# Score matmuls of a two-branch attention layer: the lower halves of q of both components in one block, on two halves of TensorE's rows

## The chip, the core and the metric

One core of a Trainium2 chip. A core has five engines that run their own instruction streams: TensorE (PE; its weight loads are shown apart as PEld), VectorE (DVE), ScalarE (ACT), GpSimd (POOL) and SyncE (SP, here the issuer of almost all DMAs). TensorE multiplies a stationary block of up to 128 rows x 128 columns with a moving block of up to 512 columns and adds into PSUM, which has eight banks. The metric is the device time of one execution in microseconds; lower is better. All times are of the whole kernel.

## What is computed

One layer of a streaming encoder: 2048 prompt rows (16 tiles of 128) and 128 sample rows (8 sequences of 16, one further tile), width 1024. After adaLN modulation one projection gives q, k, v and gates of two attention branches, A and B; both are merged, projected and normed.

```python
def diff_attention(q, k, v, qpos, kpos, lam):            # A: 4 heads, 2 components of 64
    s = jnp.einsum('bqhcd,bkhcd->bhcqk', q, k) * (HEAD_DIM_A ** -0.5)
    mask = (kpos // CHUNK)[None, :] <= (qpos // CHUNK)[:, None]
    p = jax.nn.softmax(jnp.where(mask, s, -jnp.inf), axis=-1)
    w = p[:, :, 0] - lam * p[:, :, 1]
    return jnp.einsum('bhqk,bkhe->bqhe', w, v)

def stick_breaking_attention(q, k, v, qpos, kpos):        # B: 8 heads of 64
    z = jnp.einsum('bqhd,bkhd->bhqk', q, k) * (HEAD_DIM_B ** -0.5)
    mask = kpos[None, :] < qpos[:, None]
    log_1m = jnp.where(mask, jax.nn.log_sigmoid(-z), 0.0)
    log_a = jax.nn.log_sigmoid(z) + lax.cumsum(log_1m, axis=3, reverse=True) - log_1m
    a = jnp.where(mask, jnp.exp(log_a), 0.0)
    return jnp.einsum('bhqk,bkhd->bqhd', a, v)
```

Inputs and outputs are float32. The kernel gets near that precision from float16 by halves: a value x is scaled and split into an upper half, x rounded to float16, and a lower half, the rounding error, and a product of two values is taken as upper x upper + upper x lower + lower x upper.

## The kernel before, in words

**Units.** The work is cut into eight units u of two *components* of 64 dimensions: even u is a head of A (its two components c = 0, 1), odd u two heads of B (one component each). For every unit the 17 tiles are taken in the order sample tile (t = NT = 16), then t = 0 to 15. A step is one (unit, tile).

**What a step does.** `project` (from L407) multiplies a tile of the modulated input with the unit's weights in 24 matmuls of 512 columns (L428) and, for the gates, 24 more (L504). Its `finish` splits q, k and v into halves on ScalarE (upper) and VectorE (lower): `halves` and `query`, L456 to L463. A's q and k are rotated on POOL before that. `transpose_qk` (L512) turns q and k with TensorE into one bank of PSUM (tag `t`) and copies them out (L531, L532): on ScalarE for A, on VectorE for B. `scores` (L625) goes over chunks of 512 keys, of which a tile t has t // 4 + 1, the last (diagonal) one of 128 to 512 columns with a mask that is added by one more matmul (L643). `evacuate` (L549) takes a chunk's scores out of PSUM: for A on VectorE with a running maximum (L558), for B as two sigmoids on ScalarE (L119), the second in place, which `stick` then reads in a scan on VectorE (L616). After the last chunk come softmax and weights (A: `softmax_pair`) or the products on POOL (B: `stick_weights`, L622), a split, a transpose by DMA (`turn`), and two steps later the multiplication with v (`pv_block`, L696 to L701).

**The score matmul.** `k16` holds for each component c the 128 columns [upper k | lower k], so that its transpose, block c of `kst`, has upper k on rows 0 to 63 and lower k on rows 64 to 127. `qbuf` holds four blocks of 128: for each c the upper q twice, [upper q | upper q], and for each c [lower q | zeros]; the zeros are written once at the start by POOL (L398). One matmul over 128 rows (L639) gives upper q x upper k + upper q x lower k; the second (L640), over 128 rows too, adds lower q x upper k and multiplies the lower k with zeros.

**PSUM.** Eight banks of 512 float32 columns: two of tag `mm` (projection), three of `s` (scores), one of `t` (transposes, gates), two of `o` (PV). A bank is taken in turn when `bank(tag)` is called; the first matmul into it waits until the last reader of its former content is done. In A one chunk of one component takes one `s` bank.

**Order.** `interleave` (L91) merges, for each step, three lists of pieces: projections taken from a line that runs about five steps ahead, the chunks of `scores`, and the PV blocks of the step two before. Each piece has a cost, and a piece is placed by the middle of its cost within its list's total. On top of this the framework's scheduler, which works with a model of times, may move instructions of an engine past one that is not ready in its model; on the chip each engine then runs its list in order.

**Tail.** After the eight units come the branch and output projections (L1315, L1344), and beside them the sample rows (`sample`, L722), whose q, k and v halves were put into DRAM (`s_d`, L491 and L534) during the units and are read back (`fetch`, L734). `queries` (L740) spreads the samples' q over a padded tile `qpad`, so that the scores over the cached keys run as matmuls of 32 columns of TensorE (L772); `scores_all` (L756) does these and the scores over the samples' own keys, both components of which share one `s` bank. `s` banks also serve the transposes of the tail (L1163).

Of the kernel before, what the change touches and what calls it, by code (L numbers as in the profile page):

```python
# [109 lines left out]
def layer_kernel(ctx: ExitStack, tc: tile.TileContext, a: dict):  # L110
# [54 lines left out]
    g_d = [dram.tile([P, 2 * D], F32, name=f"g_d{t}") for t in range(NT + 1)]  # L165
    s_d = [dram.tile([P, 8, P], F16, name=f"s_d{u}") for u in range(8)]
    gate_d = dram.tile([9, D], F32, name="gate_d")
# [227 lines left out]
    qs = c01.enter_context(tc.tile_pool(name="qs", bufs=1))  # L395
    qbuf = [qs.tile([P, 2, 2, 2, 64], F16, name=f"qbuf{i}") for i in range(2)]
    for qb in qbuf:
        G.memset(qb[:, 1, :, 1, :], 0.0)  # L398
    silu_z = {}
# [7 lines left out]
    def project(U, t):  # L407
# [30 lines left out]
        def finish():  # L438
# [17 lines left out]
            def halves(dst, src, scale):  # L456
                src = src.rearrange("p (c d) -> p c d", d=64)
                split(dst[:, :, 0, :], dst[:, :, 1, :], src, scale, S)

            def query(src, scale):  # L460
                src = src.rearrange("p (c d) -> p c d", d=64)
                S.activation(out=qb[:, 0, :, :, :], in_=src.unsqueeze(2).to_broadcast([P, 2, 2, 64]), func=AF.Identity, scale=scale)
                V.scalar_tensor_tensor(out=qb[:, 1, :, 0, :], in0=src, scalar=scale, in1=qb[:, 0, :, 0, :], op0=ALU.mult, op1=ALU.subtract)  # L463
            if kind == 0:
                cosT, sinT = box["r"][:, 0:32], box["r"][:, 32:96]
                x4 = pr[:, 0:256].rearrange("p (c f d) -> p c f d", c=4, f=2)
                rot = stg.tile([P, 256], F32, tag="rot", name="rot")
                r2 = stg.tile([P, 256], F32, tag="r2", name="r2", bufs=1)
                G.tensor_tensor(out=rot.rearrange("p (c f d) -> p c f d", c=4, f=2), in0=x4,
                                in1=cosT.unsqueeze(1).unsqueeze(1).to_broadcast([P, 4, 2, 32]), op=ALU.mult)  # L470
                G.tensor_tensor(out=r2.rearrange("p (c f d) -> p c f d", c=4, f=2), in0=x4[:, :, ::-1, :],
                                in1=sinT.rearrange("p (f d) -> p f d", f=2).unsqueeze(1).to_broadcast([P, 4, 2, 32]),
                                op=ALU.mult)
                G.tensor_tensor(out=rot, in0=rot, in1=r2, op=ALU.add)
                halves(vt, p[:, 256:384], s2)
                query(rot[:, 0:128], s)
                halves(k16, rot[:, 128:256], s)
            else:
                rot = pr
                halves(vt, p[:, 256:384], s2)  # L480
                halves(k16, p[:, 128:256], s2)
                query(p[:, 0:128], s2)
# [7 lines left out]
            if t == NT:  # L490
                load(out=s_d[U["u"]][:, 6:8, :], in_=vt.rearrange("p c f d -> p c (f d)"))  # L491
            U["q16", t], U["k16", t] = qb, k16
# [19 lines left out]
    def transpose_qk(U, t):  # L512
        g, i = t // 4, t % 4
        q16, k16 = U.pop(("q16", t)), U.pop(("k16", t))
        pt = bank("t", F16)
        for c in range(2):
            T.transpose(pt[:, c * P : (c + 1) * P], k16[:, c, :, :].rearrange("p f d -> p (f d)"), id16)
        for f in range(2):
            for c in range(2):
                j = 2 + f * 2 + c  # L520
                T.transpose(pt[:, j * P : (j + 1) * P], q16[:, f, c, :, :].rearrange("p r d -> p (r d)"), id16)
        if t == NT:
            sam = stg.tile([P, 6, P], F16, tag="sam", name="sam", bufs=1)
            qst, kst = sam[:, 0:4, :], sam[:, 4:6, :]
        else:
            if i == 0:
                U["k"][g] = kvp.tile([P, 2, 512], F16, tag="k", name="k", bufs=K_BUFS)
            U["q", t] = qst = stg.tile([P, 4, P], F16, tag="qst", name="qst", bufs=Q_BUFS)
# [3 lines left out]
        copy(out=qst, in_=pt[:, 256:768].rearrange("p (j n) -> p j n", j=4))  # L532
        if t == NT:
            load(out=s_d[U["u"]][:, 0:6, :], in_=sam)  # L534

# [89 lines left out]
    def scores(U, t, jobs):  # L625
# [5 lines left out]

        def chunk(c, ch):
            job = own[c if kind == 1 else 0]
            seg = job["segs"][ch * 4 // SEG]
            n = 512 if ch < t // 4 else (t % 4 + 1) * P
            p = bank("s")
            qst, kk = U["q", t], U["k"][ch]
            diag = ch == t // 4
            T.matmul(p[:, 0:n], qst[:, c, :], kk[:, c, 0:n], start=True, stop=False)  # L639
            T.matmul(p[:, 0:n], qst[:, 2 + c, :], kk[:, c, 0:n], start=False, stop=not diag)  # L640
            if diag:
                m = mask_a if kind == 0 else mask_b
                T.matmul(p[:, n - m.shape[1] : n], idb, m, start=False, stop=True)  # L643
            evacuate(job, seg, c, p, ch * 512 - seg["lo"] * P, n, sc[:, 3:4], sc[:, 4:5], ch)
            if kind == 0:
                if diag and c == 1:
# [20 lines left out]
        return ([(0.1, silu)] if kind == 1 else []) + [(2.0 if ch < t // 4 else (t % 4 + 1) / 2, lambda c=c, ch=ch: chunk(c, ch)) for c, ch in order]  # L667

# [53 lines left out]
    def sample(U, dec, qpad, cs):  # L722
# [16 lines left out]

        def queries():  # L740
            for r in range(2):
                V.tensor_copy(out=qpad.rearrange("p j (i r) n -> p j i r n", r=2)[:, :, :, r, r * NS : (r + 1) * NS],
                              in_=box["s"][:, 0:4, :].rearrange("p j (i r s) -> p j i r s", r=2, s=NS)[:, :, :, r, :])

# [11 lines left out]
        def scores_all():  # L756

            box["jobs"] = [new_job(U, t, c, 5, dec) for c in range(heads)]
            qsam, kn = box["s"][:, 0:4, :], box["s"][:, 4:6, :]
            mask = mask_as if kind == 0 else mask_bs  # L760
            pn = bank("s")
            for c in range(2):
                p = pn[:, c * P : (c + 1) * P]
                T.matmul(p, qsam[:, c, :], kn[:, c, 0:P], start=True, stop=False)
                T.matmul(p, qsam[:, 2 + c, :], kn[:, c, 0:P], start=False, stop=False)
                T.matmul(p, idb, mask, start=False, stop=True)
            for c in range(2):
                pc = bank("s")
                for b in range(2):
                    for f in range(2):  # L770
                        for i in range(4):
                            T.matmul(pc[i * 32 : i * 32 + 32, :], qpad[:, f * 2 + c, 2 * i + b, :], box["k", i][:, b * 4 : b * 4 + 4, c, :],  # L772
                                     start=(b == 0 and f == 0), stop=(b == 1 and f == 1))
                job = box["jobs"][c % heads]
                seg = job["segs"][0]
                evacuate(job, seg, c, pn[:, c * P : (c + 1) * P], 512, P, sc[:, 3:4], sc[:, 4:5], 1)
                evacuate(job, seg, c, pc, 0, 512, box["f"][:, 0:1], box["f"][:, 1:2], 0)
                if kind == 1:
                    stick(seg, None, 512, P, pn[:, c * P : (c + 1) * P])
                    stick(seg, None, 0, 512, pc)  # L780
# [27 lines left out]
        def finish():  # L808
            po = bank("s")
            vn = box["s"][:, 6:8, :].rearrange("p c (f d) -> p c f d", f=2)  # L810
            for job in box["jobs"]:
# [615 lines left out]
```

## Time and profile before

| | |
|---|---|
| median of 3 runs | 2341.11 us (2338.23 to 2343.4) |
| profiled execution: span | 2337.1 us |
| matmuls, and as many weight loads | 15272 |
| mean rate of DMA | 191 GB/s, 445.35 MB |
| score matmuls L639 and L640 | 640 each |
| transposes of k (L517) and q (L521) | 272 and 544 |

The span runs from the first to the last instruction of the profiled execution; the lowest of the runs, which are timed from outside, is 1.1 us above it, the median 4.0 us; the profiled execution has no other time of its own. L12 is line 12 of the kernel before. Busy shares are shares of the span; a matmul's shown duration is longer than its share of TensorE's time, since matmuls follow each other before the one ahead has ended, so the distance between starts is what counts for a row of matmuls.

### The profile page before, as it was taken

The numbers are of one execution on the slowest core, as the hardware profiler recorded it, in microseconds if no ns is written. First come the engines' busy times: TensorE is split into PE (matmuls) and PEld (weight loads), VectorE is DVE, ScalarE is ACT, GpSimd is POOL, SyncE is SP. The second block draws the span as 40 slices with busy tenths as digits, with TensorE's granted clock in tenths as the row PEclk, the third lists the DMA queues.
The fourth block names the chain that finished last, engine by engine and source line by source line (L and its number), as shares of the span: only waits on it lengthen the run. The fifth ranks groups of instructions, "written<-read, shape, count | busy, mean of one in ns | idle before, by whom it ended". The sixth has DMA issues, their size and how long they took to land. (4 is left out here: it accounts for less than half of the span.)

```text
span 2337.1 us, 42708 instructions
## 1 busy us (share of the span) xinstructions
PE 2121.6 (91%) x15272; PEld 1144.0 (49%) x15272; DVE 1707.5 (73%) x3653; ACT 1663.1 (71%) x3292; POOL 661.3 (28%) x578
## 2 busy tenths in 40 slices
PE   5998898998989899899999979999995878989998
PEld 3654454545545445445545545554553444544443
DVE  4658765779875677978667797777788777777663
ACT  4968777787877778778677777866777656756541
POOL 1222022356300334731024474103345111121111
PEclk7999999999999999999999999999997988999999
DMA  9777659897895898867577777756677999999521
GB/s 333 275 214 180 152 118 272 179 193 168 212 210 126 216 204 192 179 178 192 134 191 176 185 168 186 195 146 150 146 171 166 285 254 233 257 245 236 155 98 53
DMA packets 834358, 445.35 MB, mean 191 GB/s; under 512 B 537210, under 2 KB 777130, under 8 KB 833632
## 3 DMA queue, kind: packets, MB, share of 16 engines
q1 hardware_dynamic: 833196, 442.24, 76.0%
q8 instruction: 119, 1.95, 0.4%
q14 instruction: 95, 0.78, 0.1%
q10 hardware_dynamic: 948, 0.39, 0.1%
HBM read 245.60 MB, written 69.24 MB: 135 GB/s over the span
## 5 line engine op out<-in xcount | busy, mean ns | idle before, releaser
L622 POOL TENSOR_TENSOR sc_p<-sc_p,sc_n 128x127 f32<-128x127 f32 (+7 forms) x192 | 313.8, 1638 | 826.5 <-DVE sc_n L616 812.2
L428 PE MATMUL ps_mm<-wb,hs 128*128 128x512 f16 x1632 | 414.5, 382 | 1.5 <-DMA hs<-hT_d 1.3
L428 PEld LDWEIGHTS <-hs 128*128 128x128 f16 x3120 | 274.4, 98 | 257.3 <-DMA hs<-hT_d 11.8
L428 PE MATMUL ps_mm<-wa,hs 128*128 128x512 f16 x1488 | 374.6, 382 | 9.8 <-DVE qbuf L463 6.4
L616 DVE TENSOR_TENSOR_SCAN sc_n<-ps_s,sc_n,zero_t 128x512 f32<-128x512 f32 x192 | 245.4, 1278 | 68.4 <-ACT ps_s L119 65.0
L639 PE MATMUL ps_s<-k,qst 128*128 128x512 f16 (+3 forms) x640 | 224.2, 351 | 37.9 <-DVE sc_n L616 29.9
L573 DVE TENSOR_TENSOR sc_n<-sc_p,sc_n 128x128 f16<-128x128 f32 (+7 forms) x192 | 212.7, 1112 | 58.1 <-ACT sc_n L572 57.6
L504 PEld LDWEIGHTS <-hs 128*128 128x128 f16 x1632 | 156.6, 98 | 188.3 <-ACT qst L532 6.2
L119 ACT ACTIVATE sc_p<-ps_s,usc 128x512 f32<-128x512 f32 (+3 forms) x320 | 204.8, 640 | 30.2 <-PE ps_s L640 25.3
L640 PE MATMUL ps_s<-k,qst 128*128 128x512 f16 (+3 forms) x640 | 224.2, 352 | 0.0
L572 ACT CAST sc_n<-sc_p 128x128 f16<-128x128 f32 (+7 forms) x192 | 155.5, 813 | 78.5 <-POOL sc_p L622 76.9
L700 PE MATMUL ps_o<-v,wt 128*128 128x128 f16 x1088 | 171.5, 225 | 32.6 <-DMA wt<-sc_n 32.2
L119 ACT ACTIVATE ps_s<-ps_s,usc 128x512 f32<-128x512 f32 (+3 forms) x328 | 200.0, 610 | 0.0
L504 PE MATMUL ps_t<-wa,hs 128*128 128x512 f16 x816 | 192.9, 383 | 7.6 <-ACT qst L532 6.0
L504 PE MATMUL ps_t<-wb,hs 128*128 128x512 f16 x816 | 191.9, 380 | 1.2 <-DVE qst L532 0.8
L1344 PE MATMUL ps_o<-wo,wb 128*128 128x512 f16 x816 | 186.5, 383 | 4.1 <-ACT wb L1166 4.1
L701 PE MATMUL ps_o<-v,wt 128*128 128x64 f16 x1088 | 157.9, 197 | 0.0
L700 PEld LDWEIGHTS <-wt 128*128 128x128 f16 x1088 | 105.1, 101 | 98.1 <-DMA wt<-sc_n 45.1
L558 DVE TENSOR_SCALAR_CACHE_REDUCE sc_p<-ps_s,usc 128x512 f32<-128x512 f32 (+3 forms) x160 | 106.3, 665 | 42.4 <-PE ps_s L640 31.7
L616 DVE TENSOR_TENSOR_SCAN sc_n<-ps_s,zero_t 128x128 f32<-128x128 f32 (+3 forms) x128 | 104.1, 814 | 44.0 <-ACT ps_s L119 43.4
L558 DVE TENSOR_SCALAR_CACHE_REDUCE sc_n<-ps_s,usc 128x512 f32<-128x512 f32 (+3 forms) x160 | 106.3, 665 | 36.9 <-PE ps_s L640 26.3
L701 PEld LDWEIGHTS <-wt 128*128 128x128 f16 x1088 | 103.1, 100 | 54.3 <-issue 1.1
(360 smaller groups left out, 4493.6 us busy)
## 6 DMA issues: line engine op xcount, KB each, us to landing
hs<-hT_d SPq DMA_DIRECT2D x130, 512.0 KB, 4.2
g_d<-gt SPq DMA_DIRECT2D x68, 256.0 KB, 4.2
wb<-g_d SPq DMA_DIRECT2D x26, 512.0 KB, 4.8
out_dram<-pr SPq DMA_DIRECT2D x204, 64.0 KB, 2.3
o_d<-o SPq DMA_DIRECT2D x136, 64.0 KB, 2.2
hs<-o_d SPq DMA_DIRECT2D x17, 512.0 KB, 5.6
out_dram<-x SPq DMA_DIRECT2D x17, 512.0 KB, 2.8
wide<-in_w_ada_dram SPq DMA_DIRECT2D x8, 1024.0 KB
```

What stands on the lines that cost most here:

```text
L119: i = S.activation(**kw)
L428: T.matmul(box["p"], box["h"][:, hi, k, :], U["w"][k][:, wi, :], start=(n == 0), stop=(n == 3 * KT - 1))
L504: T.matmul(box["g"][:, 0:gw], box["h"][:, hi, k, :], U["wg"][k // per][:, k % per, wi, :], start=(j == 0), stop=(j == 3 * KT - 1))
L558: V.tensor_scalar(out=dst[:, lo : lo + n], in0=p[:, 0:n], scalar1=sc_pos, scalar2=None, op0=ALU.mult, op1=ALU.max, accum_out=job["mx"][:, ...
L573: V.tensor_tensor(out=lo, in0=src, in1=hi, op=ALU.subtract)
L616: V.tensor_tensor_scan(out=dst[:, lo : lo + n][:, ::-1], data0=src[:, 0:n][:, ::-1], data1=zero_t[:, 0:1].to_broadcast([P, n]), initial=fi ...
L622: G.tensor_tensor(out=p[:, 0:m], in0=p[:, 0:m], in1=n[:, 1 : m + 1], op=ALU.mult)
L639: T.matmul(p[:, 0:n], qst[:, c, :], kk[:, c, 0:n], start=True, stop=False)
L640: T.matmul(p[:, 0:n], qst[:, 2 + c, :], kk[:, c, 0:n], start=False, stop=not diag)
L700: T.matmul(po[:, c * P : (c + 1) * P], wt[:, wj, :], vt[:, c, :, :], start=first, stop=False)
L701: T.matmul(po[:, c * P : c * P + 64], wt[:, nb + wj, :], vt[:, c, 0, :], start=False, stop=last)
L1344: T.matmul(po, st["y"][:, yi * 8 + k, :], wo[j * 4 + k // 2][:, wi, k % 2, :], start=(n == 0), stop=(n == 3 * KT - 1))
```

## The change

`qbuf` gets three blocks: [upper q | upper q] for c = 0, the same for c = 1, and one block [lower q of c = 0 | lower q of c = 1]; nothing is left to be zeroed. In `k16` the halves of component 1 change places, [lower k | upper k], so that after the transpose upper k lies on rows 0 to 63 for c = 0 and on rows 64 to 127 for c = 1. The lower matmul then contracts over 64 rows, those of its component. `transpose_qk` makes five transposes for a tile where it made six, and `qst` has three blocks.

```diff
-            k16 = stg.tile([P, 2, 2, 64], F16, tag="k16", name="k16")
+            k16 = stg.tile([P, 4, 64], F16, tag="k16", name="k16")
...
+            def key(src, scale):
+                halves(k16[:, 0::3, :], k16[:, 1:3, :], src, scale)
...
-                V.scalar_tensor_tensor(out=qb[:, 1, :, 0, :], in0=src, scalar=scale, in1=qb[:, 0, :, 0, :], op0=ALU.mult, op1=ALU.subtract)
+                V.scalar_tensor_tensor(out=qb[:, 2, :, :], in0=src, scalar=scale, in1=qb[:, 0:2, 0, :], op0=ALU.mult, op1=ALU.subtract)
...
-        for f in range(2):
-            for c in range(2):
-                j = 2 + f * 2 + c
-                T.transpose(pt[:, j * P : (j + 1) * P], q16[:, f, c, :, :].rearrange("p r d -> p (r d)"), id16)
+        for j in range(3):
+            T.transpose(pt[:, (2 + j) * P : (3 + j) * P], q16[:, j, :, :].rearrange("p r d -> p (r d)"), id16)
...
-        copy(out=qst, in_=pt[:, 256:768].rearrange("p (j n) -> p j n", j=4))
+        copy(out=qst, in_=pt[:, 256:640].rearrange("p (j n) -> p j n", j=3))
```

In `scores` a piece of A now does both components of a chunk: it takes two `s` banks, issues the two upper matmuls, then the two lower ones, then mask and evacuation of each; its cost in the interleaving is that of two pieces. A piece of B is one component of one chunk as before.

```diff
-        def chunk(c, ch):
-            job = own[c if kind == 1 else 0]
-            seg = job["segs"][ch * 4 // SEG]
+        def chunk(cs, ch):
+
             n = 512 if ch < t // 4 else (t % 4 + 1) * P
-            p = bank("s")
-            qst, kk = U["q", t], U["k"][ch]
+            kk = U["k"][ch]
             diag = ch == t // 4
-            T.matmul(p[:, 0:n], qst[:, c, :], kk[:, c, 0:n], start=True, stop=False)
-            T.matmul(p[:, 0:n], qst[:, 2 + c, :], kk[:, c, 0:n], start=False, stop=not diag)
-            if diag:
-                m = mask_a if kind == 0 else mask_b
-                T.matmul(p[:, n - m.shape[1] : n], idb, m, start=False, stop=True)
-            evacuate(job, seg, c, p, ch * 512 - seg["lo"] * P, n, sc[:, 3:4], sc[:, 4:5], ch)
+            banks = {c: bank("s")[:, 0:n] for c in cs}
+            for c, p in banks.items():
+                T.matmul(p, qst[:, c, :], kk[:, c, 0:n], start=True, stop=False)
+            for c, p in banks.items():
+                rows = slice(c * 64, c * 64 + 64)
+                T.matmul(p, qst[rows, 2, :], kk[rows, c, 0:n], start=False, stop=not diag)
+            for c, p in banks.items():
+                job = own[c if kind == 1 else 0]
+                seg = job["segs"][ch * 4 // SEG]
+                if diag:
+                    m = mask_a if kind == 0 else mask_b
+                    T.matmul(p[:, n - m.shape[1] : n], idb, m, start=False, stop=True)
+                evacuate(job, seg, c, p, ch * 512 - seg["lo"] * P, n, sc[:, 3:4], sc[:, 4:5], ch)
...
-        order = [(c, ch) for ch in range(nch) for c in range(2)] if kind == 0 else \
-                [(c, ch) for c in range(2) for ch in reversed(range(nch))]
+        order = [((0, 1), ch) for ch in range(nch)] if kind == 0 else \
+                [((c,), ch) for c in range(2) for ch in reversed(range(nch))]
```

In the tail the samples' blocks are seven instead of eight; an eighth is filled by one more load per unit, which brings the lower q of c = 1 to rows 0 to 63, where the cached keys of both components have their upper half. `queries` makes four copies for two. The lower matmuls over cached keys use 64 rows, and the own-key scores of the two components lie in two `s` banks.

```diff
-            load(out=sam, in_=s_d[U["u"]])
+            load(out=sam[:, 0:7, :], in_=s_d[U["u"]])
+            load(out=sam[0:64, 7, :], in_=s_d[U["u"]][64:P, 2, :])
...
-            pn = bank("s")
-            for c in range(2):
-                p = pn[:, c * P : (c + 1) * P]
+            pn = [bank("s")[:, 0:P] for c in range(2)]
+            for c, p in enumerate(pn):
                 T.matmul(p, qsam[:, c, :], kn[:, c, 0:P], start=True, stop=False)
-                T.matmul(p, qsam[:, 2 + c, :], kn[:, c, 0:P], start=False, stop=False)
+                rows = slice(c * 64, c * 64 + 64)
+                T.matmul(p, qsam[rows, 2, :], kn[rows, c, 0:P], start=False, stop=False)
...
-                            T.matmul(pc[i * 32 : i * 32 + 32, :], qpad[:, f * 2 + c, 2 * i + b, :], box["k", i][:, b * 4 : b * 4 + 4, c, :],
+                            rows = slice(0, 64 if f else P)
+                            T.matmul(pc[i * 32 : i * 32 + 32, :], qpad[rows, f * 2 + c, 2 * i + b, :], box["k", i][rows, b * 4 : b * 4 + 4, c, :],
```

More of the change, by code (lines that the diff above doesn't have):

```diff
@@ L165, in layer_kernel @@
     g_d = [dram.tile([P, 2 * D], F32, name=f"g_d{t}") for t in range(NT + 1)]
-    s_d = [dram.tile([P, 8, P], F16, name=f"s_d{u}") for u in range(8)]
+    s_d = [dram.tile([P, 7, P], F16, name=f"s_d{u}") for u in range(8)]
     gate_d = dram.tile([9, D], F32, name="gate_d")
@@ L395, in layer_kernel @@
     qs = c01.enter_context(tc.tile_pool(name="qs", bufs=1))
-    qbuf = [qs.tile([P, 2, 2, 2, 64], F16, name=f"qbuf{i}") for i in range(2)]
-    for qb in qbuf:
-        G.memset(qb[:, 1, :, 1, :], 0.0)
+    qbuf = [qs.tile([P, 3, 2, 64], F16, name=f"qbuf{i}") for i in range(2)]
     silu_z = {}
@@ L474, in finish @@
                 G.tensor_tensor(out=rot, in0=rot, in1=r2, op=ALU.add)
-                halves(vt, p[:, 256:384], s2)
+                value(p[:, 256:384])
                 query(rot[:, 0:128], s)
-                halves(k16, rot[:, 128:256], s)
+                key(rot[:, 128:256], s)
             else:
                 rot = pr
-                halves(vt, p[:, 256:384], s2)
-                halves(k16, p[:, 128:256], s2)
+                value(p[:, 256:384])
+                key(p[:, 128:256], s2)
                 query(p[:, 0:128], s2)
@@ L490, in finish @@
             if t == NT:
-                load(out=s_d[U["u"]][:, 6:8, :], in_=vt.rearrange("p c f d -> p c (f d)"))
+                load(out=s_d[U["u"]][:, 5:7, :], in_=vt.rearrange("p c f d -> p c (f d)"))
             U["q16", t], U["k16", t] = qb, k16
@@ L527, in transpose_qk @@
                 U["k"][g] = kvp.tile([P, 2, 512], F16, tag="k", name="k", bufs=K_BUFS)
-            U["q", t] = qst = stg.tile([P, 4, P], F16, tag="qst", name="qst", bufs=Q_BUFS)
+            U["q", t] = qst = stg.tile([P, 3, P], F16, tag="qst", name="qst", bufs=Q_BUFS)
             kst = U["k"][g][:, :, i * P : (i + 1) * P]
@@ L531, in transpose_qk @@
         copy(out=kst, in_=pt[:, 0:256].rearrange("p (c n) -> p c n", c=2))
-        copy(out=qst, in_=pt[:, 256:768].rearrange("p (j n) -> p j n", j=4))
+        copy(out=qst, in_=pt[:, 256:640].rearrange("p (j n) -> p j n", j=3))
         if t == NT:
-            load(out=s_d[U["u"]][:, 0:6, :], in_=sam)
+            load(out=s_d[U["u"]][:, 0:5, :], in_=sam)
     def new_job(U, t, c, nb, pool=None):
@@ L740, in queries @@
         def queries():
+            qp = qpad.rearrange("p j (i r) n -> p j i r n", r=2)
+            qv = box["s"].rearrange("p j (i r s) -> p j i r s", r=2, s=NS)
             for r in range(2):
[L742 to L743 removed]
+                c = slice(r * NS, (r + 1) * NS)
+                V.tensor_copy(out=qp[:, 0:2, :, r, c], in_=qv[:, 0:2, :, r, :])
+                V.tensor_copy(out=qp[0:64, 2:4, :, r, c], in_=qv[0:64, 2::5, :, r, :])
         def cache(name, i):
@@ L809, in finish @@
             po = bank("s")
[L810 removed]
+            vn = box["s"][:, 5:7, :].rearrange("p c (f d) -> p c f d", f=2)
             for job in box["jobs"]:
```

26 lines of the change are left out of this document (14 added, 12 removed).

## The prediction

> **What bounds the kernel now.** I read the page first: the engines' busy shares and the forty slices.
>
> ```profile
> span 2337.1 us, 42708 instructions
> PE 2121.6 (91%) x15272; PEld 1144.0 (49%) x15272; DVE 1707.5 (73%) x3653; ACT 1663.1 (71%) x3292; POOL 661.3 (28%) x578
> ...
> PE   5998898998989899899999979999995878989998
> ...
> PEclk7999999999999999999999999999997988999999
> ```
>
> TensorE is busy 91% of the span at a clock of 0.9 or more nearly throughout; no other engine passes 73%. But busy is a modelled figure for a pipelined engine, so I went on to TensorE's busy time by stage and to who made it wait. The first stage below is head 0 of the stick-breaking branch ("B"), the second head 1 of the differential branch ("A"), the third B's head 2, the fourth A's head 3; the last is the tail, with the output projection and the sample rows.
>
> ```profile
> core 0: us, PE busy (x), PEclk, DMA share, GB/s
> ...
> 319.00:552.00 233.00, 214.68 (x1500) 0.99 0.87 199
> 552.00:728.00 176.00, 166.34 (x1169) 0.99 0.77 186
> ...
> 1161.00:1393.00 232.00, 214.50 (x1531) 0.99 0.79 181
> 1393.00:1563.00 170.00, 165.10 (x1157) 0.99 0.71 178
> ...
> 1790.00:2337.00 547.00, 480.99 (x3740) 0.92 0.77 202
> ```
>
> Not busy are 18 us of a B stage (233.00 - 214.68), 5 to 10 us of an A stage. TensorE is the bound in both; in B it also waits. The waits, in total, times and longest:
>
> ```profile
> PE ps_o L700 <- DMA wt<-sc_n: 32.2, 25, 4.8
> PE ps_s L639 <- DVE sc_n L616: 29.9, 43, 2.5
> PE ps_o L696 <- DMA wt<-sc_n: 20.4, 14, 4.2
> ...
> PE ps_s L639 <- DVE sc_p L558: 4.5, 4, 2.5
> ```
>
> The second row is the one that this change touches: at 43 of B's 320 chunks the next score matmul waits until the scan has let go of a bank of PSUM. The last row is its like in A: four waits in 320 chunks.
>
> **What TensorE's stream costs now.** Score matmuls, transposes and the sample's cached scores, by shape:
>
> ```profile
> L640 PE MATMUL ps_s<-k,qst 128*128 128x512 f16 x448 | 172.1, 384 | 0.0
> ...
> L521 PE MATMUL ps_t<-id,qbuf 128*128 128x128 f16 x544 | 55.0, 220 | 0.0
> ...
> L772 PE MATMUL ps_s<-dks,qpad 128*32 128x512 f16 x256 | 24.3, 432 | 8.5 <-DMA dks<-k16c 8.5
> ...
> L640 PE MATMUL ps_s<-k,qst 128*128 128x384 f16 x64 | 21.4, 335 | 0.0
> ...
> L640 PE MATMUL ps_s<-k,qst 128*128 128x256 f16 x64 | 17.4, 272 | 0.0
> ...
> L640 PE MATMUL ps_s<-k,qst 128*128 128x128 f16 x64 | 13.9, 220 | 0.0
> ```
>
> Durations overlap; what counts is the spacing of starts. Four full matmuls in a row took 1.03 us, one lasts 0.38, so the spacing is (1.03 - 0.38)/3 = 0.217 us at 512 columns. Four transposes took 0.39 us, one 0.22: 0.057 us at 128 columns. The diagonal chunk shows 0.16 us at 384 (1543.59 to 1543.75); 256 lies between, 0.11.
>
> ```profile
> 2319.85 1.03 PE L1344 MATMUL ps_o<-wo,wb 128*128 128x512 f16 x4
> 2320.81 1.12 PE L1303 MATMUL ps_t<-gsm,sel 9*128 9x512 f32 x2
> ...
> 95.25 0.39 PE L521 MATMUL ps_t<-id,qbuf 128*128 128x128 f16 x4
> ...
> 1543.59 0.33 PE L639 MATMUL ps_s<-k,qst 128*128 128x384 f16 x1
> ...
> 1543.75 0.33 PE L640 MATMUL ps_s<-k,qst 128*128 128x384 f16 x1
> ```
>
> **The question that decides: a matmul on 64 rows between matmuls on 128.** No 64-row matmul is in this trace. The nearest rows are matmuls that use only some of the array's rows or columns. In the fence above the fourth L1344 starts at 2319.85 + 3 x 0.217 = 2320.50, and L1303 on 9 rows not at 2320.72 but at 2320.81: 0.09 us more. The tail shows a whole round trip, into 32 columns and out:
>
> ```profile
> 1834.52 0.59 PE L1315 MATMUL ps_mm<-wb,wb 128*128 128x512 f16 x2
> 1834.95 0.38 PE L1315 MATMUL ps_mm<-wa,wb 128*128 128x512 f16 x1
> 1835.26 0.39 PE L772 MATMUL ps_s<-dks,qpad 128*32 128x512 f16 x2
> 1835.58 0.39 PE L1315 MATMUL ps_mm<-wa,wb 128*128 128x512 f16 x1
> ```
>
> L772 comes 0.31 us after its predecessor and the next full matmul 0.32 us after L772, where 0.217 is usual: 0.63 - 2 x 0.217 = **0.20 us for the round trip**, about 0.10 each way. The two L772 themselves, on different columns, last 0.39 us together, as long as one: they run side by side. That the 9-row matmul is f32 is not the reason for its delay: where f32 matmuls on all rows are followed by f16 there is none (the fourteen below are (1.73 - 0.28)/13 = 0.11 us apart, the last starts at 93.51, L428 0.11 later).
>
> ```profile
> 92.06 1.73 PE L1086 MATMUL ps_s<-diag,wide 128*128 128x128 f32 x14
> 93.62 1.67 PE L428 MATMUL ps_mm<-wa,hp 128*128 128x512 f16 x7
> ```
>
> So a partial use of rows (9) and of columns (32) both cost the array's emptying at the border. I take 0.20 us for a visit to 64 rows too. The ends: 0.0, if 64 rows are treated like 128, and 0.20; I take the upper because the row for few rows is the nearer kin and shows it.
>
> The Trainium skill, "TensorEngine Tiling (Array Packing)", section Key Properties, says that changing the tiling mode, not just the tile, drains TensorE. It speaks against this change, and the 0.09 and 0.10 us above agree with it; by it every visit pays, without it none, which is the first rival below. The same page gives no price.
>
> **The change part by part, on TensorE.**
>
> B, 320 chunks: the lower matmul has the same columns as before, so nothing is won, and each becomes a visit of its own between full-row matmuls (its upper half before it; a mask, PV or projection after it). 320 x 0.20 = **+64 us**.
>
> A, 160 pairs (112 of 512 columns, 16 each of 384, 256, 128: half of half of the counts above): two lower matmuls become two on separate halves of the rows. If they run side by side, as the columns do, one spacing goes: 112 x 0.217 + 16 x (0.16 + 0.11 + 0.057) = -29.5 us. One visit per pair comes: 160 x 0.20 = +32. Together **+2.5 us**: at 512 columns a pair gains 0.02, at 128 it loses 0.14.
>
> The Trainium skill, "TensorE: Matmul & The Clock Gate", section Measured speedup vs the span model, gives packed row tiles one matmul's time plus about 4 ns per further tile. No run here shows rows; by it the saving of 29.5 would shrink by 160 x 4 ns = 0.6 us, an estimate.
>
> A's banks: the pair holds two of the three score banks at once. Now a bank is needed again after three chunks; then the second upper matmul of a pair needs the bank of the pair before, whose reader on VectorE (L558) takes 0.75 us at 512 columns:
>
> ```profile
> 1549.53 0.75 DVE L558 TENSOR_SCALAR_CACHE_REDUCE sc_n<-ps_s,usc 128x512 f32<-128x512 f32 x1
> ...
> 1550.30 0.75 DVE L558 TENSOR_SCALAR_CACHE_REDUCE sc_p<-ps_s,usc 128x512 f32<-128x512 f32 x1
> ```
>
> Where the bank isn't free, either everything behind on TensorE (PV, projection) waits, or the order of instructions is made such that the first lower matmul goes ahead and the pair falls apart into two visits. A pair fallen apart costs its saving and one visit more: all of them 29.5 + 32 = 61.5 us, none 0. I take a quarter, **+15 us**, nearer the low end, because of the four waits for L558 above.
>
> Transposes: 17 tiles x 8 units = 136, each with one fewer: 136 x 0.057 = **-8 us**. Their copy out of PSUM shrinks from 512 to 384 columns; it takes 589 ns on ScalarE and 414 on VectorE (below), at most a quarter less, some 0.1 us x 136. Both engines stand behind TensorE, so I count 0; if that cover went, it would be -14 us at most.
>
> ```profile
> L532 ACT COPY qst<-ps_t x64: 573/589/653, 91.7 to 1502.0; 128x512 f16<-128x512 f16 x64
> L532 DVE COPY qst<-ps_t x64: 406/414/418, 278.5 to 1744.3; 128x512 f16<-128x512 f16 x64
> ```
>
> Tail: 16 own-key lower matmuls at 64 rows, a visit each, 16 x 0.20 = 3.2; the cached scores go between 128 and 64 rows inside a group, three borders more for each of 16 groups, 16 x 3 x 0.10 = 4.8: **+8 us**. The own scores hold two score banks where they held one, and these banks also serve the tail's transposes; ends 0 and eight waits of about 2 us; I take +2. One more load for each unit on SP's queue (8, of 16 KB) is needed four steps later, two more VectorE copies per unit are 16 short ones in a stage where TensorE is busy 481 of 547 us: 0. The dropped memsets were two, at the start, on POOL: 0.
>
> Sum on TensorE: 64 + 2.5 + 15 - 8 + 8 + 2 = **+83 us**.
>
> **What the waits give back.** Where TensorE waits for the scan, ScalarE and VectorE set the pace of B's chunks: two sigmoids of 0.70 and 0.68 us against one scan of 1.28 us.
>
> ```profile
> L616 DVE TENSOR_TENSOR_SCAN sc_n<-ps_s,sc_n,zero_t 128x512 f32<-128x512 f32 x48 | 61.4, 1278 | 19.1 <-ACT ps_s L119 18.2
> ...
> L119 ACT ACTIVATE sc_p<-ps_s,usc 128x512 f32<-128x512 f32 x56 | 39.2, 700 | 5.3 <-PE ps_s L640 5.0
> L119 ACT ACTIVATE ps_s<-ps_s,usc 128x512 f32<-128x512 f32 x56 | 37.9, 676 | 0.0
> ```
>
> There a later TensorE only waits less. I let all 29.9 us of that wait go, and none of the waits for transposed weights (32.2 and 20.4), whose chains start at the scores and move with them. 83 - 30 = **+53 us**, so the span becomes 2390. The page gives no time around the span; the median of the runs, 2341.11, is 4 us above it: forecast **2394 us**, by itself 2370 to 2420.
>
> **Rivals.**
>
> *No border between 64 and 128 rows.* Then the change does what its words promise: -29.5 - 8 = -37 us on an engine that is the bound, **2304 us**, a little more where VectorE's L558 then sets A's pace. For it: no 64-row matmul here says otherwise. Against it: the 9-row and the 32-column rows, both at about 0.1 us. It decides as soon as a visit costs less than (29.5 + 8)/(160 + 320 + 16) = 0.08 us. Chance 0.10.
>
> *A's pairs fall apart, or the two halves run one after the other.* The first costs 61.5 instead of 15: 2394 + 46 = **2440 us**; the second the saving alone, 2394 + 29.5 = 2423. For it: three banks, two of them held. Against it: few waits for L558 today. Chance 0.15.
>
> *B is bound by its chain.* If the pace of B were the sigmoids, the scan and the transposed weights everywhere, its 64 us would vanish in the waits (29.9 + 32.2 = 62, about as much): 83 - 62 = 21, **2362 us**. For it: the 18 us without TensorE in each B stage. Against it: 43 waits, not 320. Chance 0.15.
>
> **How the numbers follow.** Forecast 0.60, rivals 0.10, 0.15, 0.15. From 2345 to 2445 the range holds the forecast and the last two; it leaves out the first rival and small tails. Faster by over 0.2% (about what this measurement can tell from no change) has the first rival's 0.10; within 0.2% 0.03, between it and a nearly hidden B; slower 0.87.
>
> **What would show it.** Right: lower score matmuls as 64-row shapes, starting about 0.31 us after a full upper matmul, with about 0.1 us after them before the next full one; in A two of them within some ns; B stages longer by 10 to 15 us each, A stages by 0 to 6; fewer waits of L639's successor for L616. Wrong: 0.217 us at those borders (first rival); lower matmuls of a pair apart, with an L558 wait or other work between (second); B stages of unchanged length (third).

## The result, and the profile after

| | before | after |
|---|---|---|
| median of 4 runs | 2340.29 us (2338.23 to 2343.4) | 2399.68 us (2393.29 to 2405.41) |
| span of the profiled execution | 2337.1 us | 2397.8 us |

The ratio is 1.0248 (95% interval 1.0231 to 1.0266): 58 us slower by this ratio (59 by the medians), and 6 us beyond the forecast of 2394. The page of the changed kernel, engines first, then TensorE by slices:

```profile
span 2397.8 us, 42477 instructions
PE 2233.3 (93%) x15136; PEld 1105.4 (46%) x15136; DVE 1724.8 (72%) x3669; ACT 1664.5 (69%) x3292; POOL 666.0 (28%) x576
...
PE   5998998998999899899999999999997889989998
```

TensorE has 136 matmuls fewer and is busy 112 us longer. Where the time went is seen at the lower matmul, now on 64 rows (groups by shape; the number after the bar is busy time, then the mean in ns):

```profile
L645 PE MATMUL ps_s<-k,qst 64*128 64x512 f16 x448 | 162.3, 397 | 0.0
...
L522 PE MATMUL ps_t<-id,qbuf 128*128 128x128 f16 x408 | 46.8, 220 | 0.1
```

Its duration looks as before (384 ns before, 397 now). The borders show in the distances between the starts. The timeline of TensorE (start, duration, line, tiles, shape, count) at a chunk of B:

```profile
1244.02 0.38 PE L642 MATMUL ps_s<-k,qst 128*128 128x512 f16 x1
1244.34 0.39 PE L645 MATMUL ps_s<-k,qst 64*128 64x512 f16 x1
1244.65 0.28 PE L642 MATMUL ps_s<-k,qst 128*128 128x256 f16 x1
1244.87 0.28 PE L645 MATMUL ps_s<-k,qst 64*128 64x256 f16 x1
1245.08 0.23 PE L651 MATMUL ps_s<-masks,idb 128*128 128x128 bf16 x1
```

From upper to lower 0.32 us, from lower to the next 0.31, where 0.217 was usual; at 256 columns 0.22 and 0.21 in place of 0.11. Over all full-width chunks the medians of the distances between starts are 312 ns on the way in and 319 ns on the way out, 216 being usual; at 128 columns they are 152 and 159, 56 being usual. So a visit costs 0.096 + 0.103 = **0.20 us**, as taken from the 9-row and the 32-column matmuls, and independent of the columns.

The weight loads of the same chunk (PEld) show what is different at a border:

```profile
1243.81 0.10 PEld L642 LDWEIGHTS <-qst 128*128 128x128 f16 x1
1244.33 0.09 PEld L645 LDWEIGHTS <-qst 64*128 64x128 f16 x1 [0.42 <-issue]
1244.65 0.10 PEld L642 LDWEIGHTS <-qst 128*128 128x128 f16 x1 [0.23 <-issue]
```

The first load starts 0.21 us before its matmul (1244.02), beside the matmul ahead. The load for the 64 rows starts 0.01 us before its own (1244.34), and the next full load together with its own (1244.65): on neither side of the visit is a load done ahead. Whether the load waits for the matmul ahead, or both for something else, isn't shown.

In A, two kinds of pairs are found. Here is one of each from head 3, the first together, the second fallen apart:

```profile
1482.58 0.59 PE L642 MATMUL ps_s<-k,qst 128*128 128x512 f16 x2
1483.11 0.39 PE L645 MATMUL ps_s<-k,qst 64*128 64x512 f16 x2
1483.43 0.34 PE L642 MATMUL ps_s<-k,qst 128*128 128x384 f16 x1
1483.70 0.33 PE L645 MATMUL ps_s<-k,qst 64*128 64x384 f16 x1
1483.96 0.20 PE L651 MATMUL ps_s<-masks,idb 128*128 128x64 bf16 x1
...
1486.87 1.89 PE L426 MATMUL ps_mm<-wb,hs 128*128 128x512 f16 x8
1488.60 0.33 PE L642 MATMUL ps_s<-k,qst 128*128 128x384 f16 x1
1488.86 0.33 PE L645 MATMUL ps_s<-k,qst 64*128 64x384 f16 x1
```

At 1483.11 the two lower matmuls together last 0.39 us, as long as one: the halves of the rows do run side by side, 3 or 4 ns apart. The diagonal chunk of 384 columns comes in two parts, at 1483.43 and, after other work, at 1488.60: the first lower matmul went ahead of the second upper one. Counted over the trace, 53 of 160 pairs stand together and 107 fell apart, so there are 320 + 53 + 2 x 107 = 587 visits, and 587 x 0.20 = 117 us of borders in the prompt's scores, 64 in B and 53 in A.

The stages (columns: length, TensorE's busy time and number of instructions, clock, DMA), bounded as those of before:

```profile
core 0: us, PE busy (x), PEclk, DMA share, GB/s
325.00:567.00 242.00, 231.06 (x1512) 0.99 0.83 191
567.00:749.00 182.00, 174.94 (x1139) 0.99 0.76 181
1194.00:1432.00 238.00, 230.27 (x1501) 0.99 0.76 176
1432.00:1612.00 180.00, 174.40 (x1151) 0.99 0.71 169
1847.00:2397.80 550.80, 490.60 (x3740) 0.93 0.77 201
```

B's stages are 9 and 6 us longer (233 and 232 before), although each has 80 visits or 16 us of borders; not busy are 11 and 8 us, which were 18 before. A's are 6 and 10 us longer, the last window 4. And the waits of TensorE:

```profile
PE ps_o L708 <- DMA wt<-sc_n: 23.6, 16, 3.2
PE ps_s L642 <- DVE sc_n L617: 14.2, 23, 1.9
PE ps_o L704 <- DMA wt<-sc_n: 11.4, 10, 1.8
```

The wait for the scan is 14.2 us (29.9 before), and the waits for transposed weights have shrunk as well, from 52.6 to 35.0 us together.

### The profile page after: what moved, and what is told of

Read it like the earlier page. It is cut to its first block, busy times and chain, and to the rows that moved or that the text cites. A ratio compares the mean times of both kernels' runs of the same rounds, so it can differ in the third digit from the quotient of the medians.

```text
span 2397.8 us, 42477 instructions
## 1 busy us (share of the span) xinstructions
PE 2233.3 (93%) x15136; PEld 1105.4 (46%) x15136; DVE 1724.8 (72%) x3669; ACT 1664.5 (69%) x3292; POOL 666.0 (28%) x576
## 5 line engine op out<-in xcount | busy, mean ns | idle before, releaser
L426 PEld LDWEIGHTS <-hs 128*128 128x128 f16 x3120 | 269.3, 98 | 260.5 <-issue 25.8
L426 PE MATMUL ps_mm<-wa,hs 128*128 128x512 f16 x1488 | 369.2, 381 | 8.4 <-DMA hs<-hT_d 4.3
L574 DVE TENSOR_TENSOR sc_n<-sc_p,sc_n 128x128 f16<-128x128 f32 (+7 forms) x192 | 217.7, 1139 | 36.9 <-ACT sc_n L573 36.2
L642 PE MATMUL ps_s<-k,qst 128*128 128x512 f16 (+3 forms) x640 | 220.5, 358 | 22.1 <-DVE sc_n L617 14.2
L507 PEld LDWEIGHTS <-hs 128*128 128x128 f16 x1632 | 153.4, 98 | 186.5 <-issue 12.5
L645 PE MATMUL ps_s<-k,qst 64*128 64x512 f16 (+3 forms) x640 | 213.6, 364 | 0.0
L645 PEld LDWEIGHTS <-qst 64*128 64x128 f16 x640 | 54.7, 93 | 210.8 <-issue 205.7
L708 PEld LDWEIGHTS <-wt 128*128 128x128 f16 x1088 | 106.8, 103 | 80.9 <-DMA wt<-sc_n 29.3
L559 DVE TENSOR_SCALAR_CACHE_REDUCE sc_n<-ps_s,usc 128x512 f32<-128x512 f32 (+3 forms) x160 | 106.4, 666 | 51.8 <-PE ps_s L645 27.6
L559 DVE TENSOR_SCALAR_CACHE_REDUCE sc_p<-ps_s,usc 128x512 f32<-128x512 f32 (+3 forms) x160 | 106.5, 666 | 49.7 <-PE ps_s L645 30.0
```

The source lines that it names most:

```text
L426: T.matmul(box["p"], box["h"][:, hi, k, :], U["w"][k][:, wi, :], start=(n == 0), stop=(n == 3 * KT - 1))
L507: T.matmul(box["g"][:, 0:gw], box["h"][:, hi, k, :], U["wg"][k // per][:, k % per, wi, :], start=(j == 0), stop=(j == 3 * KT - 1))
L559: V.tensor_scalar(out=dst[:, lo : lo + n], in0=p[:, 0:n], scalar1=sc_pos, scalar2=None, op0=ALU.mult, op1=ALU.max, accum_out=job["mx"][:, ...
L574: V.tensor_tensor(out=lo, in0=src, in1=hi, op=ALU.subtract)
L642: T.matmul(p, qst[:, c, :], kk[:, c, 0:n], start=True, stop=False)
L645: T.matmul(p, qst[rows, 2, :], kk[rows, c, 0:n], start=False, stop=not diag)
```

## The experiments

All ratios are to the kernel before, run on the same chip; the runs stand on two chips, the ninth to eleventh on the second. There it took 2345 to 2347 us.

**Without any border.** The first run gives the lower matmuls all rows and keeps the rest.

```diff
-                rows = slice(c * 64, c * 64 + 64)
+                rows = slice(0, P)
                 T.matmul(p, qst[rows, 2, :], kk[rows, c, 0:n], start=False, stop=not diag)
...
-                            rows = slice(0, 64 if f else P)
+                            rows = slice(0, P)
```

> The changed kernel with every lower matmul contracting over all 128 rows instead of 64 (in the tail too); three q blocks, five transposes, two score banks per piece of A and the order of pieces stay. The 64 rows that the change left out bring in lower q of the one component times lower k of the other, a product of two rounding errors. Theory 1 (each visit to 64 rows costs TensorE about 0.20 us at its two borders): no borders are left, starts of L645 follow those of L642 by 0.217 us at 512 columns, and the time is that of before less the transposes' 8 us plus 0 to 10 for the paired banks: 2330 to 2345 us. Theory 2 (the pieces of A that hold two of three banks cost the time that A's stages lost, 23 us): 2355 to 2370.

Measured: 2361.04 us, ratio 1.0057 (1.0037 to 1.0076). The timeline shows the usual 0.217 again, at a pair of head 3:

```profile
1449.97 0.59 PE L642 MATMUL ps_s<-k,qst 128*128 128x512 f16 x2
1450.40 0.59 PE L645 MATMUL ps_s<-k,qst 128*128 128x512 f16 x2
1450.83 0.33 PE L642 MATMUL ps_s<-k,qst 128*128 128x384 f16 x1
```

The four matmuls start within 1450.83 - 1449.97 = 0.86 us, four times 0.217. Of the 0.0248 the borders are 0.0191 (45 us). TensorE's busy time fell from 2233.3 to 2114.9 us, so 118 us on TensorE show as 45 in the time. A remainder of 0.0057 (13 us) needs another cause; by the prediction it should have been a gain. The time lies in the range of theory 2, which the next run tests.

**Without the pairs too.**

```diff
-                if diag:
+                if diag and cs[-1] == 1:
                     softmax_pair(job)
...
-        order = [((0, 1), ch) for ch in range(nch)] if kind == 0 else \
+        order = [((c,), ch) for ch in range(nch) for c in range(2)] if kind == 0 else \
...
-            pn = [bank("s")[:, 0:P] for c in range(2)]
+            pn = bank("s")
+            pn = [pn[:, c * P : (c + 1) * P] for c in range(2)]
```

> The first run's kernel, and beside it A takes one component of a chunk per piece and one score bank again, as before the change, and the samples' own scores share one bank again: of the change only the three q blocks, five transposes and the shorter copy remain. Theory 1: before less 136 transposes of 0.057 us, if TensorE is the bound all along: 2330 to 2336 us. Theory 2: the same, but 20 us or more below the first run. A third possibility, that the transposes are hidden in waits: 2338 to 2342.

Measured: 2359.12 us, ratio 1.0047 (1.0032 to 1.0062), slower than all three expectations. Theory 2 wanted 20 us between the first run and this one, and there are 2: as long as a pair may fall apart, two banks held at once don't show. The remainder is still there, in a kernel that is nearly the one of before with 136 transposes fewer (the swapped halves of k and the tail's loads and copies stay). Its waits:

```profile
PE ps_o L708 <- DMA wt<-sc_n: 42.4, 30, 6.7
PE ps_o L704 <- DMA wt<-sc_n: 28.8, 19, 4.3
PE ps_s L642 <- DVE sc_n L617: 24.4, 34, 2.4
PE ps_mm L426 <- DMA hs<-hT_d: 12.4, 9, 3.5
```

TensorE waits 71.2 us for transposed weights (52.6 before) and 12.4 us for the projection's input.

**Only A's borders, only B's borders.** In the third run B's lower matmuls have 128 rows, in the eighth A's:

```diff
-                rows = slice(c * 64, c * 64 + 64)
+                rows = slice(0, P) if kind == 1 else slice(c * 64, c * 64 + 64)
```

```diff
-                rows = slice(c * 64, c * 64 + 64)
+                rows = slice(0, P) if kind == 0 else slice(c * 64, c * 64 + 64)
```

> The changed kernel with the lower matmuls of B's prompt chunks alone on 128 rows; A and the tail stay as changed. Theory 1 with half of B's borders given back by its waits (B's four stages were 33 us longer together): 2362 to 2372 us. If every border counts in full (320 x 0.20 us): about 2336. If B was bound by its own chain and lost nothing to borders: 2395 to 2400.

> The changed kernel with the lower matmuls of A's prompt chunks alone on 128 rows; B and the tail stay at 64. If the borders of A and B add up (changed kernel 1.0248, without any border 1.0057, without B's 1.0149): 1.0248 - (1.0149 - 1.0057) = 1.016. If A's two-bank pieces cost time of their own: below the sum of the parts, 1.019 or more.

Measured: 2383.3 us, ratio 1.0149 (1.0133 to 1.0164), above the bounds that I gave, which left the remainder out; and 2384.48 us, ratio 1.0154 (1.0126 to 1.0181), as worked out. B's borders are worth 1.0248 - 1.0149 = 0.0099 (23 us, of 64 on TensorE), A's 1.0248 - 1.0154 = 0.0094 (22 us, of 53, with one spacing saved in 53 pairs). They add up. The list of TensorE's matmuls isn't quite the changed kernel's in these runs: by tiles and columns it differs at 1543 of 15136 places in the first run, 1580 in the third and 1543 in the eighth, mostly in the tail (in the third run all but four). So these shares can hold a little of what another order is worth; the ninth run below is free of that.

**Pairs held together.** One more rule of order for the scheduler:

```diff
                 upper = T.matmul(p, qst[:, c, :], kk[:, c, 0:n], start=True, stop=False)
...
                 lower = T.matmul(p, qst[rows, 2, :], kk[rows, c, 0:n], start=False, stop=not diag)
+                tc.add_manual_dep(lower.ins, upper.ins.name, NOSYNC, reason="pair")
```

> The changed kernel with one more rule for the order of instructions: a lower matmul of A may not go ahead of the second upper one, so that the lower matmuls of a pair stand next to each other in 157 of 160 pairs instead of 53. Theory 1: 104 visits and 104 spacings fewer, 104 x (0.20 + 0.19) = 41 us less on TensorE, half to all of it in the time: 2358 to 2380 us. Theory 2: the pair now waits for its second bank with nothing sent ahead: 2400 or more.

Measured: 2434.84 us, ratio 1.0379 (1.0356 to 1.0402). Theory 2 was right here. 157 pairs stand together, the two lower matmuls 3 or 4 ns apart, and 104 visits are gone; but VectorE waits longer for A's scores. The longest waits of the maximum over a chunk's scores, L559 (who waited, for whom, us, times, longest), first this kernel, then the changed one:

```profile
DVE sc_p L559 <- PE ps_s L645: 95.2, 51, 5.3
DVE sc_p L559 <- PE ps_s L652: 38.9, 25, 3.8
```

```profile
DVE sc_p L559 <- PE ps_s L645: 30.0, 28, 2.9
DVE sc_n L559 <- PE ps_s L645: 27.6, 24, 3.9
DVE sc_n L559 <- PE ps_s L651: 22.4, 17, 3.8
```

All in all the prompt's L559 waits 134.1 us for score and mask matmuls, where it was 98.6. TensorE is busy 13 us less (2220.5), where 41 were expected, and is not busy for 211.6 us in place of 164.5; it waits for L559 16 times, not 4. The likely reason: with three score banks a pair's second bank comes free only when VectorE has read the pair before, and as the lower matmuls of both must wait for the second upper one, VectorE has nothing to read in that time. The granted clock is lower too, 0.947 in place of 0.963; how much of the loss is the clock's was not taken apart. Letting the first lower matmul go ahead costs a visit and is the better choice here.

**Is it the chip?** The kernel before, unchanged:

> The kernel before, unchanged, for a trace from the same chip as the other experiments. If the residual 11 to 13 us of the first two experiments were the chip's, its tail (543 us in the first trace) and its waits for transposed weights (52.6 us) should be longer here too; if not, they are as in the first trace and the residual belongs to the kernels.

Measured: 2350.24 us, one run, among the 2343.11 to 2354.97 of its neighbours. From its last score matmul to the end it takes 559.5 us (552.7 in the first trace, counted the same way), its waits for transposed weights are 35.9 + 21.0 = 56.9 us (52.6). So on this chip the tail is longer by some us and the waits are nearly as they were: the 71.2 us of the second run belong to that kernel. There TensorE is not busy for 235.2 us (2357.9 - 2122.7), here for 226.6, and it is busy no less (2122.7 and 2121.9), although 136 transposes are gone.

**The sixth transpose back,** in the second run's kernel; its result is not used.

```diff
-        for j in range(3):
-            T.transpose(pt[:, (2 + j) * P : (3 + j) * P], q16[:, j, :, :].rearrange("p r d -> p (r d)"), id16)
+        for j in range(4):
+            T.transpose(pt[:, (2 + j) * P : (3 + j) * P], q16[:, min(j, 2), :, :].rearrange("p r d -> p (r d)"), id16)
...
-        copy(out=qst, in_=pt[:, 256:640].rearrange("p (j n) -> p j n", j=3))
+        copy(out=qst, in_=pt[:, 256:768].rearrange("p (j n) -> p j n", j=4))
```

> The second experiment's kernel (128 rows, one component per piece) with a sixth transpose, of the third q block again, and the copy of 512 columns back; its result is not used. If the 11 us that the second experiment lost came from the shorter list of transposes (another order of instructions, not TensorE time), this one has the ratio 1.000 to 1.002; if they come from what else is left of the change (the swapped halves of k, the tail's extra loads and copies), 1.004 to 1.008.

Measured: 2349.94 us (10 runs), ratio 1.0010 (0.9991 to 1.0029). The remainder is gone when work is added, and the waits for transposed weights are 60.8 us (41.4 + 19.4) in place of 71.2. What it changes is the order: leaving the transposes of q out of the lists, TensorE's matmuls (by tiles and shape) are those of the kernel before at 14690 of 14728 places with six transposes, and at 9137 with five (second run), where the lists part at the 325th. The scheduler sorts by its model of times, and 136 short instructions fewer give another list from near its start. The lists of the other engines were not compared. It follows, too, that the swapped halves of k, the tail's additional load and copies and the other edits cost nothing that can be measured.

**The tail of before,** again in the second run's kernel. An eighth block for the sample tile, made by two short transposes:

```diff
+            for r in range(2):
+                T.transpose(pt[r * 64 : r * 64 + 64, 5 * P : 6 * P], q16[:, 2, 1 - r, :], id16)
...
-            load(out=sam[:, 0:7, :], in_=s_d[U["u"]])
-            load(out=sam[0:64, 7, :], in_=s_d[U["u"]][64:P, 2, :])
+            load(out=sam, in_=s_d[U["u"]])
```

> The second experiment's kernel with the tail of before: the sample tile gets an eighth block [lower q of c = 1 | lower q of c = 0] from two more transposes of 64 columns, so that its load is one and its copies are two again. If the residual was the tail's: ratio 0.998 to 1.001. If it is the order of the main part: 1.003 to 1.006 as in the second experiment.

Measured: 2375.97 us, ratio 1.0119 (1.0094 to 1.0144), outside both expectations. The tail isn't the place of the remainder: from the last score matmul to the end it takes 552.0 us here, 560.5 in the second run. Against that run this edit of eight of 136 steps moved the time by 17 us, and the loss lies in the units. From the first score matmul of an A unit to that of the B unit behind it, the units 2, 4 and 6 take 581 us together in place of 563: TensorE is not busy 7 us longer and busy 11 us longer, at a granted clock of 0.96 to 0.97 in place of 0.98 to 0.99. So this order costs waits and clock; what lowered the clock was not tested.

**The border alone.** To the kernel with six transposes, one edit:

```diff
-                rows = slice(0, P)
+                rows = slice(c * 64, c * 64 + 64)
```

> The sixth experiment's kernel, whose matmuls stand at the same places as before the change in 14783 of 14821 cases, with one edit: the prompt's 640 lower matmuls contract over 64 rows. The order of instructions stays the same to the last one, no two lower matmuls stand together, so this is the border alone: 640 x 0.20 = 128 us on TensorE. If the waits give back the same share as between the changed kernel and the first experiment (0.019 of the time, 45 us, for 587 visits of 117 us): ratio 1.001 + 0.021 = 1.022. If every border counts: 1.055. If none does: 1.001.

Measured: 2417.98 us, ratio 1.0299 (1.0277 to 1.0321), 0.0289 above the kernel without borders and between the expected 1.022 and the 1.055 of borders that all count: 68 us for 640 visits of 128 us (the two kernels ran on two chips, each against the kernel before there). TensorE's list is the same at all 15272 places, so this is the price of the borders and not of an order: 53% of what TensorE pays. TensorE's busy time is 128.9 us longer (2248.4 against 2119.5), and the time in which it isn't busy 62.2 shorter (168.0 against 230.2). TensorE's waits, first without borders, then with them:

```profile
PE ps_o L709 <- DMA wt<-sc_n: 41.4, 39, 4.9
PE ps_s L643 <- DVE sc_n L618: 25.5, 38, 2.1
PE ps_o L705 <- DMA wt<-sc_n: 19.4, 15, 3.5
```

```profile
PE ps_o L709 <- DMA wt<-sc_n: 25.3, 24, 4.8
PE ps_s L643 <- DVE sc_n L618: 17.0, 23, 1.9
...
PE ps_o L705 <- DMA wt<-sc_n: 8.5, 6, 2.8
```

Of the 60 us that don't show in the time, these three rows give 16.1 + 8.5 + 10.9 = 35.5. And the same four stages, B, A, B, A, of both:

```profile
316.00:555.00 239.00, 217.62 (x1521) 0.99 0.86 194
555.00:729.00 174.00, 164.35 (x1157) 0.99 0.78 188
1160.00:1395.00 235.00, 217.70 (x1537) 0.99 0.79 182
1395.00:1566.00 171.00, 163.44 (x1163) 1.00 0.74 174
```

```profile
327.00:571.00 244.00, 233.56 (x1536) 0.99 0.83 191
571.00:756.00 185.00, 180.89 (x1164) 0.99 0.75 177
1200.00:1444.00 244.00, 233.97 (x1553) 1.00 0.76 175
1444.00:1626.00 182.00, 178.76 (x1159) 1.00 0.70 164
```

Each stage has 80 visits, 16 us. A's stages, with 8 to 10 us not busy, grow by 11; B's, with 17 to 21 not busy, by 5 to 9. In these four stages, the more a stage waits, the less of a border is seen.

**Other orders with five transposes.**

```diff
-LEAD = 5.0
+LEAD = 4.5
```

(in the eleventh run `LEAD = 6.0`)

> The second experiment's kernel (128 rows, five transposes) with the projections running 4.5 instead of 5 steps ahead. If its ratio of 1.0047 and the seventh's of 1.0119 are accidents of the order that the scheduler made, another lead gives another order and another ratio, anywhere from 0.997 to 1.012; with the full gain of the transposes it would be 0.997.

> The same with 6 steps ahead: anywhere from 0.997 to 1.012 if it is the order; if it is something of the kernel itself (swapped halves of k, tail), 1.004 to 1.006 again.

Measured: 2366.59 us, ratio 1.0088 (1.0062 to 1.0115), and 2364.49 us, ratio 1.0083 (1.0063 to 1.0103). All five kernels with five transposes and no border lie between 1.0047 and 1.0119, none at the 0.997 that the work alone would give. Another order gives another time, as expected. Why all are slower stays open, and so does which lead or place of the transposes would give an order as good as that of before; what another lead does to the kernel before was not run, so the lead's own share in these two isn't known. No version here beats the kernel before; the one with six transposes and full rows equals it.

## Why the prediction was right, point by point

*The border, 0.20 us for a visit to 64 rows, taken from matmuls on 9 rows and 32 columns:* right, 0.096 in and 0.103 out, and the first rival (no border) is out. The row of 9 rows showed only the way in, and f32 was ruled out there by a change from f32 to f16, the other direction; the kernel before has the usual 216 ns from f16 to f32 on all rows as well (L428 to L1086). The rule of the Trainium skill, "TensorEngine Tiling (Array Packing)", section Key Properties, that a change of the tiling mode drains TensorE, agrees with these two numbers for 64 rows too.

*B, 320 visits, +64 us on TensorE:* right as to TensorE; in the time they are 23 us (changed kernel against third run). B's two stages grew by 9 and 6 us, below the 10 to 15 that were to show it, and A's by 6 and 10, at or above the 0 to 6: the total was split wrongly between the branches.

*A, two lower matmuls side by side:* right, 3 or 4 ns apart where they stand together. The Trainium skill, "TensorE: Matmul & The Clock Gate", section Measured speedup vs the span model, has about 4 ns for a further tile; the trace agrees.

*A's pairs, a quarter fallen apart, +15 us:* mis-sized. 107 of 160 fell apart, which is 61.5 x 107/160 = 41 us. The few waits for L558 that I went by say how long TensorE waited on the chip; the scheduler orders by its model, in which the second bank may often be still taken; that this is why it let the first lower matmul go ahead is argued, but the fourth run fits: with that forbidden, TensorE waits for L559 16 times, not 4. The second rival's mechanism was thus the common case. Its price in the time was not: A's borders cost 22 us, and holding the pairs together cost more than letting them go.

*Transposes, -8 us; banks of the tail, +2; its borders, +8:* the work went (408 transposes of q for 544), the gain did not come. The run with the sixth transpose back points to why: fewer instructions made another order, and without any border it was 13 us slower. This is the step that the prediction lacked. From the last score matmul to the end it takes 555.7 us, 3 more than before (552.7); the kernel before on the experiments' chip takes 559.5, so the tail's small terms can't be told apart.

*The waits give back 30 us, those for the scan and none for transposed weights:* mis-sized, and wrong as to which. The scan's wait gave 15.7, the weights' 17.6, and with the same order the borders lost 47% to waits. The chains behind the transposed weights were not as tied to TensorE's own pace as I took them to be: with a slower TensorE these waits shrank too.

*The sum, 83 - 30 = 53:* 58 measured. With what the runs show: 117 us of visits less 10 for 53 saved spacings and 8 in the tail are 115 on TensorE, of which 45 show in the time, and 13 come from the order. The mechanism, a border at each visit that the waits hide in part, was right; that the sum comes within 6 us is in part luck: more border and more cover are off in opposite directions, and the order's 13 us stand where a gain of 8 was forecast.

*The third rival, B bound by its chain:* half right: B's 64 us became 23, not 0.

## What to carry to other kernels

A matmul on part of TensorE's rows between matmuls on all of them pays two borders (0.20 us together here), so contracting over 64 rows is only worth it when more time is saved side by side within a visit than its two borders cost; look for the border in any partial matmul of the trace before, and multiply by visits, not by matmuls. Two halves that are to run side by side need both of their PSUM banks free at the same moment, and must stand together in the order that is really issued. Where a scheduler orders by a model, taking out instructions is a new order, and a gain of less than a per cent has to be measured against a run that puts the work back without its use.

## What was not expected of the hardware

The price of the border hardly depends on how the matmul is partial: 64 rows cost 0.096 us on the way in and 0.103 on the way out, at 128 columns as at 512; 32 columns cost 0.094 and 0.096 in the kernel before (medians of the distances, 310 and 312 ns), and 9 rows in f32 0.093 on the way in (309). On the way out of the 9 rows no border can be told from the f32 matmul's own 0.53 us. The shown duration of the matmul hides it (397 ns against 384), and TensorE's busy share even rises (93% from 91%), since the shown durations still overlap at a border (0.38 us shown where the starts are 0.32 apart).

The weight load stops running ahead at a border. Over all 512-column chunks of the changed kernel the median load for 64 rows starts 4 ns before its own matmul and 308 ns after the start of the matmul ahead; on full rows (sixth run) it starts 214 ns before its own and 2 ns after the start of the one ahead.
